# FFN input products of 512 tokens as one matmul instruction instead of two, first layer split 520 + 520, output gates for 1024 tokens

## The chip, the cores and the metric

The kernel runs on one core of one Trainium2 chip. The metric is the time of one launch on the device, in microseconds (us). Three runs of the kernel before gave 1883.02, 1883.82 and 1885.05 us; the median is 1883.82 us.

## What is computed

A trunk of one residual layer over 1024 tokens of width 1024, ahead of which 16 learned meta tokens are put (1040 tokens, dropped again at the end). All of it is float32:

```python
h = concat(meta, x)
h = h + 0.5 * rmsnorm(swiglu(rmsnorm(h, g0), w_in[0], w_out[0]), g1)      # first FFN, d_ff = 2816
h = h + rmsnorm(mlstm_mixer(rmsnorm(h, g2)), g3)                          # conv, gates, scan, output gate
h = h + 0.5 * rmsnorm(swiglu(rmsnorm(h, g4), w_in[1], w_out[1]), g5)      # second FFN
# swiglu(x): gu = x @ w_in ; (silu(gu[:, :2816]) * gu[:, 2816:]) @ w_out
```

In the mixer, the output of the scan is multiplied with sigmoid(og), og being 1024 columns of the projected input: that is the output gate. It is needed only for the 1024 real tokens.

## The kernel before

Activations stand transposed (width on the 128 partitions, tokens along the free dimension), weights are the stationary operand and tokens the moving one. Every float32 product is made of three passes on fp32r operands: each operand is split in a high part (ScalarE cast) and a low part (VectorE subtraction), and hi*hi, hi*lo and lo*hi are added in PSUM (`PASSES`, line 40).

The tokens are worked in two halves. Before the change these are A, 528 tokens (16 meta and 512 real), and B, 512 tokens, in the first FFN and the mixer, and C and E, 512 each, in the second FFN (lines 74 and 75). A matmul writes at most 512 columns, so 528 tokens go as two matmuls of 264 into the two banks of a 1024-column PSUM tile.

**The input products of an FFN** (gate and up, `x @ w_in`) are not made directly. One level of the Strassen-Winograd scheme is used: with two halves of the width, two halves of the tokens, and gate and up, each of the 22 tiles of 128 columns of d_ff takes seven products instead of eight. An operand of each product is a block of tokens, or a sum or difference of blocks of both halves of the tokens, so both halves are brought to one length; b0.n is 528 in the first FFN, with B padded with 16 zero columns (line 522), and 512 in the second. `heads` (line 428) makes two of the seven for all 22 tiles and writes them to DRAM (`hd`), while `operands` (line 494) builds the other five operands piece by piece on VectorE and ScalarE from pieces that POOL's queue loads (line 508). `joint` (line 445) loads the two back and makes the other five for each tile; VectorE adds them up, the finished activations of A leave after the fourth of them (line 484), those of B after the fifth (line 490), both by POOL's queue, into two DRAM tiles `ad[0]` and `ad[1]`. Each product is made by `product` (line 407): 4 blocks of the half width, 3 passes, and always two matmuls of n/2 columns for the two halves of n:

```python
for k in range(4):
    for pi, (wp_, xp_) in enumerate(PASSES):
        for s in range(2):
            pe.matmul(ps[:, s * 512 : s * 512 + m], lhsT=w[:, wp_, k * P : (k + 1) * P],
                      rhs=x[:, xp_, k, s * m : (s + 1) * m], ...)
    if k % 2:
        tick()
```

So one product is 24 matmuls, a layer has 22 * 7 = 154 products, and the two layers have 7392 such matmuls: 3696 of 264 columns and 3696 of 256.

**The output products** (`down`, line 560) read the activations back (`load_a`, line 553, by SP's queue, split on ScalarE and VectorE) in three segments of tiles (14 to 21, 0 to 7, 8 to 13; `SEGS`, line 238). They run for A with two matmuls of 264, for B, C and the first half of E with one of 512 or 256. The first segment of A is loaded while `joint` runs (`first_a`, line 653).

**The output gates** (`out_gates`, line 857) are eight products of 128 columns each over all tokens of a half, through `fm` (line 716): for A two matmuls of 264 for each of 24 steps, the 16 meta tokens among them, for B one of 512. Sigmoid runs on ScalarE, and POOL's queue writes the real tokens to `ogd`.

**Order of the work.** Weights come through a queue of their own, `order`: SP loads raw tiles (4 in flight), `next_w` splits them, and up to 5 split tiles stand ready. Work beside the matmuls is put in `tasks` as generators; `tick` takes one step of it, twice in each product and once in two k-steps elsewhere, so that its instructions are laid among those of the matmuls. Each engine and each queue works its instructions in order; the framework may put instructions that wait for nothing earlier than the program names them. At the start SP loads the A half of x in four pieces of two blocks (lines 623 and 627), then B's (line 640), and lines 634 to 637 build the first two operands.

Of the kernel before, what the change touches and what calls it, by code (L numbers as in the profile page):

```python
# [20 lines left out]
F32 = mybir.dt.float32  # L21
# [21 lines left out]
class Half:  # L43


    def __init__(self, i, n, meta=0, s0=0):
        self.i, self.n, self.meta, self.s0 = i, n, meta, s0
        self.subs = [(0, n)] if n <= 512 else [(0, n // 2), (n // 2, n - n // 2)]

    def part(self, s0, n):  # L50
        return Half(self.i, n, 0, self.s0 + s0)


@with_exitstack
def trunk(ctx: ExitStack, tc: tile.TileContext, xa, xb, w1, w2, w2t, g5, wqk, wv, wog, wo, par, cst, out):
    nc = tc.nc
    vec, act, pool, pe, sp = nc.vector, nc.scalar, nc.gpsimd, nc.tensor, nc.sync

# [12 lines left out]
        es = ExitStack()  # L71
        return es, es.enter_context(tc.tile_pool(name=name, bufs=bufs, reuse_waits="tile"))

    A, B = Half(0, 528, NMETA), Half(1, 512, 0)
    C, E = Half(0, 512), Half(1, 512)


    def slot(i, name):
# [13 lines left out]
    convb = pk[:, 80:88]  # L92
    ident = cp.tile([P, P], F32, name="ident")
    ones = cp.tile([P, 1], F32, name="ones")
    rn = [cp.tile([P, h.n], F32, name=f"rn{h.i}") for h in (A, B)]
    vec.memset(ones, 1.0)
    act.activation(cp.tile([P, 1], F32, name="table"), ones, AF.Silu)

    h1 = [dram.tile([P, KT, 512], F32, name=f"h1_{i}") for i in range(2)]
    h2 = [dram.tile([P, KT, 512], F32, name=f"h2_{i}") for i in range(2)]  # L100
    ad = [dram.tile([NF, P, 528], F32, name=f"a_{i}") for i in range(2)]
    hd = dram.tile([NF, 2, P, 528], F32, name="hd")
    xn = dram.tile([P, KT, 512], F32, name="xn")
    vd = dram.tile([9, P, D], F32, name="vd")
# [299 lines left out]
    def shaped(t, n):  # L404
        return t[:, :n].rearrange("p (s c) -> p s c", s=2) if n > 512 else t[:, :n]

    def product(ps, w, x, m, first):
        for k in range(4):
            for pi, (wp_, xp_) in enumerate(PASSES):
                for s in range(2):  # L410
                    pe.matmul(  # L411
                        ps[:, s * 512 : s * 512 + m],
                        lhsT=w[:, wp_, k * P : (k + 1) * P],
                        rhs=x[:, xp_, k, s * m : (s + 1) * m],
                        start=(first and k == 0 and pi == 0),
                        stop=(k == 3 and pi == 2),
                        skip_group_check=True,
                    )
            if k % 2:
                tick()  # L420

    def pv(ps, n):
        return ps.rearrange("p (s c) -> p s c", s=2)[:, :, : n // 2]

    def tv(t, n):
        return t[:, :n].rearrange("p (s c) -> p s c", s=2)

    def heads(fs, X, n, scaled):


        for f in fs:
            w = next_w()
            t, c = tmp("ht"), tmp("hc")
            x = bank("hx")
            product(x, w[0], X[0], n // 2, True)
            act.copy(tv(t, n), pv(x, n))
            pool.dma_start(hd[f, 0, :, :n], t[:, :n])
            y = bank("hy")
            product(y, w[1], X[1], n // 2, True)
            vec.tensor_tensor(tv(c, n), tv(t, n), pv(y, n), ALU.add)  # L440
            if scaled:
                act.activation(c[:, :n], c[:, :n], AF.Silu)
            pool.dma_start(hd[f, 1, :, :n], c[:, :n])

    def joint(fs, X, b0, b1, r, then):


        n = b0.n
        m = n // 2
        kept = {}  # L450

        def fetch_head(f):
            u, g = tmp("u"), tmp("g")
            sp.dma_start(u[:, :n], hd[f, 0, :, :n])
            sp.dma_start(g[:, :n], hd[f, 1, :, :n])
            kept[f] = u, g

        p = 0
        fetch_head(fs[0])
        for i, f in enumerate(fs):  # L460
            v, c = tmp("v"), tmp("c")
            u, g = kept.pop(f)
            z = bank("pz", p)
            product(z, next_w()[0], X[4], m, True)
            if r is not None:
                vec.tensor_tensor(u[:, :n], u[:, :n], r[:, :n], ALU.mult)
                vec.tensor_tensor(g[:, :n], g[:, :n], r[:, :n], ALU.mult)
                act.activation(g[:, :n], g[:, :n], AF.Silu)
            vec.tensor_tensor(tv(u, n), tv(u, n), pv(z, n), ALU.add)
            then(f, 6)  # L470
            w = bank("pw", 1 - p)
            product(w, next_w()[0], X[5], m, True)
            vec.tensor_tensor(tv(v, n), tv(u, n), pv(w, n), ALU.add)
            then(f, 7)
            if i + 1 < len(fs):
                fetch_head(fs[i + 1])
            y = bank("py", p)
            product(y, next_w()[0], X[3], m, True)
            vec.tensor_tensor(tv(v, n), tv(v, n), pv(y, n), ALU.add)
            then(f, 5)  # L480
            product(w, next_w()[0], X[6], m, False)
            vec.tensor_tensor(tv(c, n), tv(u, n), pv(w, n), ALU.add)
            vec.tensor_tensor(g[:, :n], g[:, :n], c[:, :n], ALU.mult)
            pool.dma_start(ad[0][f, :, :n], g[:, :n])
            then(f, 4)
            product(y, next_w()[0], X[2], m, False)
            vec.tensor_tensor(tv(u, n), tv(u, n), pv(y, n), ALU.add)
            act.activation(u[:, :n], u[:, :n], AF.Silu)
            vec.tensor_tensor(v[:, :n], v[:, :n], u[:, :n], ALU.mult)
            pool.dma_start(ad[1][f, :, : b1.n], v[:, : b1.n])  # L490
            then(f, 3)
            p = 1 - p

    def operands(src, b0, b1, gi, X, normed, bp, name):
# [18 lines left out]
        for k in range(4):  # L513
            for i, j in ((1, k), (1, k + 4), (0, k), (0, k + 4)):
                m = (b0, b1)[i].n
                q = t[i, j]
                if i or not normed:
                    vec.scalar_tensor_tensor(
                        q[:, :m], q[:, :m], gains[:, gi, j : j + 1], rn[i][:, :m], ALU.mult, ALU.mult)
                    yield  # L520
                if m < n:
                    vec.memset(q[:, m:n], 0.0)
                if (i, j) == (1, k + 4):
                    put(2, k, q[:, :n])
                    yield
# [24 lines left out]

    alp = [None]

    def load_a(b, fs, dst):
        for i, f in enumerate(fs):
            t = alp[0].tile([P, 528], F32, name="al", tag="al")
            sp.dma_start(t[:, : b.n], ad[b.i][f, :, : b.n])
            split_to(dst[i // 4][:, 0, i % 4, : b.n], dst[i // 4][:, 1, i % 4, : b.n], t[:, : b.n])
            yield

    def down(b, fs, a, first, load=None, each=None):  # L560
# [59 lines left out]
    sp.dma_start(pk, par)  # L620
    Z = list(range(7))
    R[0] = block(Z[5], "xa")
    sp.dma_start(R[0][:, 0:2], xa[:, 0:2])
    limit[0] = 1
    fetch()
    for k in (2, 4, 6):
        sp.dma_start(R[0][:, k : k + 2], xa[:, k : k + 2])
    limit[0] = 4
    fetch()
    sp.dma_start(ident, cst[:, 0:128])  # L630
# [1 line left out]
    X[0], X[1] = operand(Z[0], "x0_0"), operand(Z[1], "x0_1")  # L632

    for k in range(KT):
        x, g, o = R[0][:, k], gains[:, 0, k : k + 1], X[k // 4]
        act.activation(o[:, 0, k % 4], x, AF.Copy, scale=g)
        vec.scalar_tensor_tensor(o[:, 1, k % 4], x, g, o[:, 0, k % 4].bitcast(F32), ALU.mult, ALU.subtract)
    R[1] = block(Z[6], "xb")
    for k in range(0, KT, 2):
        sp.dma_start(R[1][:, k : k + 2, :512], xb[:, k : k + 2])  # L640

    def operands0():
        yield from rstd(lambda k: R[0][:, k], A.n, 1.0, "n00", [], True, rn[0])
        yield from rstd(lambda k: R[1][:, k, :512], B.n, 1.0, "n01", [], True, rn[1])
        for i in range(2, 7):
            X[i] = operand(Z[i], f"x0_{i}")
        yield from operands((xa, xb), A, B, 0, X, False, bp, "o0")

    tasks.append(operands0())
    heads(TILES, X, A.n, False)  # L650
    finish()

    def first_a(li, b, Z):
        a0 = []

        def then(f, q):
            if f == 0 and q == 6:
                a0.extend((operand(Z[0], f"a{li}_0"), operand(Z[1], f"a{li}_1")))
                tasks.append(load_a(b, SEGS[0], a0))

        return a0, then

    es_b.close()
    es_al, alp[0] = stage("al0", 2)
    a0, then = first_a(0, A, Z)
    joint(TILES, X, A, B, rn[0], then)
    finish()
    es_al.close()
    es.close()
# [23 lines left out]
    if True:  # L693
# [22 lines left out]
        def fm(h, name, every=2):  # L716
# [3 lines left out]
            for k in range(KT):  # L720
                for pi, (wp_, xp_) in enumerate(PASSES):
                    for s, (s0, m) in enumerate(h.subs):
                        pe.matmul(  # L723
                            ps[:, s * 512 : s * 512 + m],
                            lhsT=w[k // 4][:, wp_, k % 4 * P : (k % 4 + 1) * P],
                            rhs=xh[h.i][k // 4][:, xp_, k % 4, s0 : s0 + m],
                            start=(k == 0 and pi == 0),
                            stop=(k == KT - 1 and pi == 2),
                        )
# [125 lines left out]
                    tasks.appendleft(gates(h, gates_t, got))  # L855

        def out_gates(h):
            n = h.n
            for c in range(KT):
                ps = fm(h, f"wog{h.i}_{c}")  # L860
                e = tmp("oge")
                act.activation(sbv(h, e[:, :n]), psv(h, ps), AF.Sigmoid)
                pool.dma_start(
                    ogd[4 * h.i : 4 * h.i + 4, :, c].rearrange("c p t -> p c t"),
                    e[:, h.meta : n].rearrange("p (c t) -> p c t", t=P),
                )

        taken = {}
# [315 lines left out]
def _layout(inputs):  # L1184
# [4 lines left out]
    def tiles(w):  # L1189
# [17 lines left out]
    cst[0:8, [256] + [256 + 16 + 128 * c for c in range(4)]] = 0.0  # L1207
    cst[0:8, [256 + 528 + 128 * c for c in range(4)]] = 0.0
    return {
        "xa": xt[:, :, :528], "xb": xt[:, :, 528:], "w1": w1, "w2": w2,  # L1210
        "w2t": f["ffn_w_out"][0, 1].reshape(NF, P, D), "g5": f["norm_gains"][0, 5:6], "wqk": tiles(wa[:, 0:1024]), "wv": wv,
        "wog": tiles(wa[:, 2048:3072]), "wo": tiles(f["a_w_out"][0]), "par": par, "cst": cst,
    }
# [19 lines left out]
```

## Time and profile before

| what | value |
|---|---|
| median of 3 runs | 1883.82 us |
| the profiled execution | 1881.98 us, its span 1880.2 us |
| TensorE busy / weight loads busy | 1853.1 us / 1738.7 us |
| VectorE / ScalarE / GpSimd busy | 1294.1 / 768.3 / 209.8 us |
| mean granted TensorE clock | 0.998 of full speed |

The span reaches from the first to the last instruction of the profiled execution; 1.8 us of its time lie outside it. PE is TensorE's matmuls, PEld its weight loads (each matmul has one, and it overlaps the matmul ahead), DVE is VectorE, ACT ScalarE, POOL GpSimd, SP SyncE; a name with q (SPq, POOLq) is that engine's queue of DMA issues. The ends of matmuls are modelled in the profile, so that one matmul's duration includes its way through the array; the pace is read from a stretch's length over its number of matmuls. A few per cent of the matmul records can be missing, and a window's count takes in those that overlap its edges, so that counts come from the program.

### The profile page before, as it was taken

What the parts mean: (1) busy time and instruction counts of PE and PEld (TensorE: products, weight loads), DVE (VectorE), ACT (ScalarE), POOL (GpSimd) and SP (SyncE); (2) the same over time, 40 slices, a digit from 0 to 9 for tenths busy, and PEclk for the clock granted to TensorE, in tenths of its full rate; (3) what the DMA queues carried; (4) which work ended last, traced back from release to release, by engine and by line L of the source; (5) the groups of instructions that cost most, each with busy time, mean ns of one, the idle gap of its engine ahead of it and who ended that gap; (6) DMA issues with size and microseconds to landing.
All of it is one profiled execution on the core that took longest, in us unless ns stands there. A gap on an engine that the chain in (4) does not pass through costs nothing.

```text
span 1880.2 us, 34386 instructions
## 1 busy us (share of the span) xinstructions
PE 1853.1 (99%) x13556; PEld 1738.7 (92%) x13556; DVE 1294.1 (69%) x2310; ACT 768.3 (41%) x1352; POOL 209.8 (11%) x376
## 2 busy tenths in 40 slices
PE   7999999999999999999999999999999999999998
PEld 7999999999999888899789878999999999888996
DVE  6857888887356746772864577787788777545874
ACT  5433333323334423443555445564233222344553
POOL 1210000000000101301002112221000000000200
PEclk9999999999999999999999999999999999999999
DMA  8555444445346424624435546766555444554863
GB/s 311 200 202 177 165 166 153 142 145 182 116 153 192 154 79 150 194 91 139 129 109 168 180 132 228 253 230 208 163 169 174 146 160 144 180 161 142 302 203 123
DMA packets 113218, 320.23 MB, mean 170 GB/s; under 512 B 14512, under 2 KB 23152, under 8 KB 113056
## 3 DMA queue, kind: packets, MB, share of 16 engines
q1 hardware_dynamic: 84032, 223.09, 37.8%
q0 software_dynamic: 28880, 94.67, 14.1%
q8 instruction: 107, 1.75, 0.4%
q14 instruction: 55, 0.45, 0.1%
q10 hardware_dynamic: 144, 0.26, 0.0%
HBM read 248.09 MB, written 69.88 MB: 169 GB/s over the span
## 4 chain that ended last, share of the span: by engine, by line
PE 91%; issue 4%; DMA 2%; DVE 1%; ACT 1%; POOL 1%; DVEq 0%; POOLq 0%; ACTq 0%
PE pd L568 23%; PE py L411 13%; PE pw L411 13%; PE pz L411 7%; PE hy L411 6%; PE hx L411 6%; PE po L999 5%; PE wog_ps L723 5%; PE wqk_ps L723 4%; PE pv L834 4%; PE pt L1126 3%; PE pn L946 1%; DMA o<-xa 1%; DMA W<-nmd 1%; PE pn L940 0%
## 5 line engine op out<-in xcount | busy, mean ns | idle before, releaser
L568 PE MATMUL pd<-a,w 128*128 128x264 f32 (+2 forms) x2592 | 433.2, 328 | 0.0
L568 PEld LDWEIGHTS pd<-a,w 128*128 128x128 f32 x2592 | 383.7, 188 | 46.1
L411 PE MATMUL py<-x,w1j_p 128*128 128x264 f32 (+1 forms) x2112 | 266.7, 282 | 0.0
L411 PE MATMUL pw<-x,w1j_p 128*128 128x264 f32 (+1 forms) x2112 | 266.7, 282 | 0.0
L411 PEld LDWEIGHTS pw<-x,w1j_p 128*128 128x128 f32 x2112 | 258.4, 188 | 0.0
L411 PEld LDWEIGHTS py<-x,w1j_p 128*128 128x128 f32 x2112 | 258.3, 188 | 0.0
L139 ACT CAST w1j_p<-w1j_s 128x512 fp32r<-128x512 f32 x176 | 109.4, 621 | 311.9 <-PE py L411 184.3
L140 DVE TENSOR_TENSOR w<-w_raw,w 128x512 fp32r<-128x512 f32 x192 | 123.6, 646 | 122.8 <-ACT w L139 122.2
L139 ACT CAST w<-w_raw 128x512 fp32r<-128x512 f32 x192 | 111.9, 585 | 177.4 <-PE pd L568 160.6
L411 PE MATMUL hx<-x,w1a 128*128 128x264 f32 (+1 forms) x1056 | 137.5, 286 | 10.2 <-ACT w1a L139 8.1
L411 PEld LDWEIGHTS hx<-x,w1a 128*128 128x128 f32 x1056 | 131.9, 191 | 10.9 <-ACT w1a L139 8.1
L411 PE MATMUL hy<-x,w1a 128*128 128x264 f32 (+1 forms) x1056 | 135.5, 283 | 3.0 <-DVE hc L440 2.7
L411 PEld LDWEIGHTS hy<-x,w1a 128*128 128x128 f32 x1056 | 130.0, 189 | 3.7 <-DVE hc L440 3.1
L411 PE MATMUL pz<-x,w1j_p 128*128 128x264 f32 (+1 forms) x1056 | 133.4, 282 | 0.0
L140 DVE TENSOR_TENSOR w1j_p<-w1j_s,w1j_p 128x512 fp32r<-128x512 f32 x176 | 121.9, 693 | 12.1 <-ACT w1j_p L139 10.4
L411 PEld LDWEIGHTS pz<-x,w1j_p 128*128 128x128 f32 x1056 | 129.2, 188 | 0.0
L834 PE MATMUL pv<-wv,xh 128*128 128x260 f32 (+1 forms) x864 | 108.3, 286 | 0.0
L834 PEld LDWEIGHTS pv<-wv,xh 128*128 128x128 f32 (+1 forms) x864 | 102.8, 179 | 3.8 <-issue 0.3
L723 PE MATMUL wqk_ps<-xh,wqk 128*128 128x264 f32 (+1 forms) x576 | 98.0, 325 | 0.0
L999 PE MATMUL po<-xh,wo 128*128 128x512 f32 x384 | 96.3, 400 | 0.0
L723 PE MATMUL wog_ps<-xh,wog 128*128 128x264 f32 (+1 forms) x576 | 91.8, 321 | 0.0
L723 PEld LDWEIGHTS wog_ps<-xh,wog 128*128 128x128 f32 x576 | 82.6, 188 | 8.3
(371 smaller groups left out, 2372.2 us busy)
## 6 DMA issues: line engine op xcount, KB each, us to landing
w1j_raw<-w SPq DMA_DIRECT2D x88, 512.0 KB, 3.7
w_raw<-w SPq DMA_DIRECT2D x64, 512.0 KB, 3.8
w1a_raw<-w SPq DMA_DIRECT2D x43, 512.0 KB, 4.7
al<-a SPq DMA_DIRECT2D x66, 256.0 KB, 3.7
w_raw<-w SPq DMA_DIRECT2D x32, 384.0 KB, 3.3
a<-v POOLq DMA_DIRECT2D x44, 256.0 KB, 2.5
w2t_raw<-w2t SPq DMA_DIRECT2D x22, 512.0 KB, 4.3
wv_raw<-wv SPq DMA_DIRECT2D x16, 520.0 KB, 3.5
```

The lines of the kernel that those rows point to most:

```text
L139: act.copy(t[:, 0, :n], src)
L140: vec.tensor_tensor(t[:, 1, :n], src, t[:, 0, :n].bitcast(F32), ALU.subtract)
L411: pe.matmul(ps[:, s * 512 : s * 512 + m], lhsT=w[:, wp_, k * P : (k + 1) * P], rhs=x[:, xp_, k, s * m : (s + 1) * m], start=(first and k = ...
L568: pe.matmul(ps[:, s * 512 : s * 512 + m], lhsT=w[i // 4][:, wp_, i % 4 * P : (i % 4 + 1) * P], rhs=a[i // 4][:, xp_, i % 4, b.s0 + s0 : b. ...
L723: pe.matmul(ps[:, s * 512 : s * 512 + m], lhsT=w[k // 4][:, wp_, k % 4 * P : (k % 4 + 1) * P], rhs=xh[h.i][k // 4][:, xp_, k % 4, s0 : s0 ...
L834: pe.matmul(ps[:L, :VW], lhsT=xh[h.i][k // 4][:, xp_, k % 4, t0 : t0 + L], rhs=w[k // 2][:, wp_, k % 2 * VW : (k % 2 + 1) * VW], start=(k ...
L946: pe.matmul(pn[e][:, j * 129 : (j + 1) * 129], lhsT=W[:, q], rhs=v[:, q, 0:129], start=False, stop=True, skip_group_check=True)
L999: pe.matmul(ps[:, :512], lhsT=w[k // 4][:, wp_, k % 4 * P : (k % 4 + 1) * P], rhs=xh[h.i][k // 4][:, xp_, k % 4, 0:512], start=(k == 0 and ...
L1126: pe.matmul(pt[t][h], lhsT=c[g][j // 4][:, xp_, j % 4, 256 + t * P : 256 + (t + 1) * P], rhs=w[h][:, wp_, :512], start=(i == 0 and pi == 0 ...
```

## The change

`product` takes the number of tokens and makes one matmul of n columns where n is at most 512, two of n/2 above. In the first FFN the 1040 tokens are cut 520 + 520 (F and G) for the input products, without padding; the output products and the mixer keep 528 + 512 (A and B). x comes as one array of 1040 tokens, of which both cuts are views, and the activations go to one DRAM tile `ad` of 1040 tokens a row. So the last 8 tokens of A belong to G: `load_a` fetches the first segment of A with 520 tokens a row and then these 8 tokens of all 8 tiles in one DMA of POOL's queue ("edge"), with two small splits behind it. The output gates of A are made for its 512 real tokens, as one matmul of 512. The diff, cut to its core:

```diff
+    F, G = Half(0, 520), Half(1, 520, off=520)
+    A, B = Half(0, 528, NMETA), Half(1, 512, off=528)
+    C, E = Half(0, 512), Half(1, 512, off=512)
+    xa, xb = xs[:, :, : A.n], xs[:, :, A.n :]
+    xf, xg = xs[:, :, : F.n], xs[:, :, F.n :]
...
-    ad = [dram.tile([NF, P, 528], F32, name=f"a_{i}") for i in range(2)]
+    ad = dram.tile([NF, P, T], F32, name="ad")
...
-    def product(ps, w, x, m, first):
+    def product(ps, w, x, n, first):
+        subs = 1 if n <= 512 else 2
+        m = n // subs
         for k in range(4):
             for pi, (wp_, xp_) in enumerate(PASSES):
-                for s in range(2):
+                for s in range(subs):
                     pe.matmul(
...
-            pool.dma_start(ad[0][f, :, :n], g[:, :n])
+            pool.dma_start(ad[f, :, :n], g[:, :n])
...
-            pool.dma_start(ad[1][f, :, : b1.n], v[:, : b1.n])
+            pool.dma_start(ad[f, :, n : 2 * n], v[:, :n])
...
-                if m < n:
-                    vec.memset(q[:, m:n], 0.0)
...
-    def load_a(b, fs, dst):
+    def load_a(b, fs, dst, n=None):
+        n = n or b.n
         for i, f in enumerate(fs):
             t = alp[0].tile([P, 528], F32, name="al", tag="al")
-            sp.dma_start(t[:, : b.n], ad[b.i][f, :, : b.n])
-            split_to(dst[i // 4][:, 0, i % 4, : b.n], dst[i // 4][:, 1, i % 4, : b.n], t[:, : b.n])
+            sp.dma_start(t[:, :n], ad[f, :, b.off : b.off + n])
+            split_to(dst[i // 4][:, 0, i % 4, :n], dst[i // 4][:, 1, i % 4, :n], t[:, :n])
+            yield
+        if n < b.n:
+            for _ in range(4):
+                yield
+            t = st.tile([P, len(fs), b.n - n], F32, name="edge", tag="edge", bufs=1)
+            pool.dma_start(t, ad[fs[0] : fs[-1] + 1, :, b.off + n : b.off + b.n].rearrange("f p t -> p f t"))
+            yield
+            for j in range(0, len(fs), 4):
+                o = dst[j // 4][:, :, :, n : b.n]
+                split_to(o[:, 0], o[:, 1], t[:, j : j + 4])
             yield
...
-    sp.dma_start(R[0][:, 0:2], xa[:, 0:2])
+    sp.dma_start(R[0][:, 0:2, : F.n], xf[:, 0:2])
...
-        sp.dma_start(R[1][:, k : k + 2, :512], xb[:, k : k + 2])
+        sp.dma_start(R[1][:, k : k + 2, : G.n], xg[:, k : k + 2])
...
-        yield from operands((xa, xb), A, B, 0, X, False, bp, "o0")
+        yield from operands((xf, xg), F, G, 0, X, False, bp, "o0")
...
-    heads(TILES, X, A.n, False)
+    heads(TILES, X, F.n, False)
...
-    a0, then = first_a(0, A, Z)
-    joint(TILES, X, A, B, rn[0], then)
+    a0, then = first_a(0, A, Z, F.n)
+    joint(TILES, X, F, G, rn[0], then)
...
-                            rhs=xh[h.i][k // 4][:, xp_, k % 4, s0 : s0 + m],
+                            rhs=xh[h.i][k // 4][:, xp_, k % 4, h.s0 + s0 : h.s0 + s0 + m],
...
         def out_gates(h):
-            n = h.n
+            q, n = Half(h.i, 512, 0, h.meta), 512
             for c in range(KT):
-                ps = fm(h, f"wog{h.i}_{c}")
+                ps = fm(q, f"wog{h.i}_{c}")
                 e = tmp("oge")
-                act.activation(sbv(h, e[:, :n]), psv(h, ps), AF.Sigmoid)
+                act.activation(e[:, :n], psv(q, ps), AF.Sigmoid)
```

The reading of PSUM follows (`pv` and `tv` take one block of n columns where n is at most 512), and the first two normalizing rows, the loops over x at the start and the operands of the first FFN are 520 wide instead of 528 and 512.

## Rows read from the trace of the kernel before

**Rows 1.** The page: span and busy time of each engine.

```profile
span 1880.2 us, 34386 instructions
...
PE 1853.1 (99%) x13556; PEld 1738.7 (92%) x13556; DVE 1294.1 (69%) x2310; ACT 768.3 (41%) x1352; POOL 209.8 (11%) x376
```

**Rows 2.** Stretches: length, busy PE, PEld, DVE, ACT, POOL (instructions), PEclk, DMA share, GB/s.

```profile
8.00:34.50 26.50, 23.96 (x165) 22.93 (x166) 19.59 (x39) 17.27 (x33) 2.72 (x5) 1.00 0.99 386
34.50:83.40 48.90, 46.20 (x377) 45.56 (x376) 41.31 (x78) 23.49 (x42) 11.94 (x22) 1.00 0.64 214
...
150.90:471.57 320.67, 320.67 (x2643) 320.67 (x2641) 268.17 (x402) 105.64 (x169) 23.32 (x43) 1.00 0.49 161
...
1309.41:1619.82 310.41, 310.41 (x2643) 310.41 (x2642) 239.83 (x358) 92.57 (x149) 23.86 (x44) 1.00 0.51 166
...
1619.82:1742.26 122.44, 122.44 (x531) 99.15 (x530) 60.69 (x95) 49.33 (x86) 2.04 (x4) 1.00 0.48 149
...
839.70:886.32 46.62, 46.62 (x385) 46.62 (x385) 14.52 (x23) 15.85 (x26) 5.29 (x7) 1.00 0.44 133
...
1140.80:1158.49 17.69, 17.69 (x79) 14.35 (x78) 17.48 (x28) 11.50 (x22) 4.55 (x7) 1.00 0.56 188
...
977.00:1012.90 35.90, 35.90 (x301) 35.90 (x301) 15.04 (x43) 14.94 (x30) 6.78 (x13) 1.00 0.51 163
```

**Rows 3.** PE in order of time (start, us): the mixer's output product, line 999.

```profile
1140.80 17.85 PE L999 MATMUL po<-xh,wo 128*128 128x512 f32 x76
```

**Rows 4.** PE's groups by shape (busy us, mean ns | idle before, releasers): heads, first FFN.

```profile
L411 PE MATMUL hx<-x,w1a 128*128 128x264 f32 x528 | 71.7, 292 | 10.2 <-ACT w1a L139 8.1 <-ACT x L636 2.0
L411 PE MATMUL hy<-x,w1a 128*128 128x264 f32 x528 | 69.2, 286 | 3.0 <-DVE hc L440 2.7 <-DVE x L637 0.2
```

**Rows 5.** PE in order of time, heads of the first FFN; idle time in brackets.

```profile
69.23 3.16 PE L411 MATMUL hy<-x,w1a 128*128 128x264 f32 x24 [0.43 <-DVE hc L440]
...
83.41 3.20 PE L411 MATMUL hy<-x,w1a 128*128 128x264 f32 x24 [2.27 <-DVE hc L440]
```

**Rows 6.** The chain that ended last, one step in the same stretch.

```profile
73.77 5.61 DMA o<-xa
```

**Rows 7.** POOL's DMA issues: by line, then in order of time, ninth tile of joint.

```profile
L863 POOL DMA_DIRECT2D ogd<-oge x16 | 12.1, 759 | 105.5 <-ACT oge L862 105.5
...
267.11 0.54 POOL L484 DMA_DIRECT2D a<-g  x1 [10.38 <-DVE g L483]
270.74 0.54 POOL L490 DMA_DIRECT2D a<-v  x1 [3.09 <-DVE v L489]
```

**Rows 8.** DMA issues by line: KB each, median us to landing.

```profile
a<-v POOLq DMA_DIRECT2D x44, 256.0 KB, 2.5
...
g<-hd SPq DMA_DIRECT2D x22, 264.0 KB, 4.1
a<-g POOLq DMA_DIRECT2D x22, 264.0 KB, 3.7
...
xa<-xa SPq DMA_DIRECT2D x4, 528.0 KB, 11.8
```

**Rows 9.** PE in order of time, then the stretch around it: the granted clock dips.

```profile
773.75 6.06 PE L834 MATMUL pv<-wv,xh 128*128 128x260 f32 x36
...
727.00:793.00 66.00, 64.03 (x520) 60.02 (x518) 51.35 (x123) 29.72 (x62) 23.24 (x43) 0.97 0.59 185
```

**Rows 10.** What the DMA queue of SP waited for (us, times, longest).

```profile
SPq L556 <- DMA a<-g: 75.2, 16, 5.1
```

**Rows 11.** SP's queue, then DVE, in order of time, second tile of joint.

```profile
167.42 0.33 SPq L556 DMA_DIRECT2D al<-a  x1
...
169.26 0.37 SPq L455 DMA_DIRECT2D g<-hd  x1
...
175.75 0.70 DVE L467 TENSOR_TENSOR g<-g,rn 128x528 f32<-128x528 f32 x1
```

More of the change, by code (lines that the diff above doesn't have):

```diff
@@ L43, with __init__, trunk @@
 class Half:
-    def __init__(self, i, n, meta=0, s0=0):
-        self.i, self.n, self.meta, self.s0 = i, n, meta, s0
+    def __init__(self, i, n, meta=0, s0=0, off=0):
+        self.i, self.n, self.meta, self.s0, self.off = i, n, meta, s0, off
         self.subs = [(0, n)] if n <= 512 else [(0, n // 2), (n // 2, n - n // 2)]
     def part(self, s0, n):
-        return Half(self.i, n, 0, self.s0 + s0)
+        return Half(self.i, n, 0, self.s0 + s0, self.off)
 @with_exitstack
-def trunk(ctx: ExitStack, tc: tile.TileContext, xa, xb, w1, w2, w2t, g5, wqk, wv, wog, wo, par, cst, out):
+def trunk(ctx: ExitStack, tc: tile.TileContext, xs, w1, w2, w2t, g5, wqk, wv, wog, wo, par, cst, out):
     nc = tc.nc
@@ L72, in stage @@
         return es, es.enter_context(tc.tile_pool(name=name, bufs=bufs, reuse_waits="tile"))
-    A, B = Half(0, 528, NMETA), Half(1, 512, 0)
-    C, E = Half(0, 512), Half(1, 512)
+    F, G = Half(0, 520), Half(1, 520, off=520)
[3 more added lines that the diff above has]
+    xf, xg = xs[:, :, : F.n], xs[:, :, F.n :]
     def slot(i, name):
@@ L94, in trunk @@
     ones = cp.tile([P, 1], F32, name="ones")
-    rn = [cp.tile([P, h.n], F32, name=f"rn{h.i}") for h in (A, B)]
+    rn = [cp.tile([P, h.n], F32, name=f"rn{h.i}") for h in (A, G)]
     vec.memset(ones, 1.0)
@@ L422, in pv @@
     def pv(ps, n):
-        return ps.rearrange("p (s c) -> p s c", s=2)[:, :, : n // 2]
+        return ps[:, :n] if n <= 512 else ps.rearrange("p (s c) -> p s c", s=2)[:, :, : n // 2]
     def tv(t, n):
-        return t[:, :n].rearrange("p (s c) -> p s c", s=2)
+        return shaped(t, n)
     def heads(fs, X, n, scaled):
@@ L434, in heads @@
             x = bank("hx")
-            product(x, w[0], X[0], n // 2, True)
+            product(x, w[0], X[0], n, True)
             act.copy(tv(t, n), pv(x, n))
@@ L438, in heads @@
             y = bank("hy")
-            product(y, w[1], X[1], n // 2, True)
+            product(y, w[1], X[1], n, True)
             vec.tensor_tensor(tv(c, n), tv(t, n), pv(y, n), ALU.add)
@@ L448, in joint @@
         n = b0.n
-        m = n // 2
         kept = {}
@@ L463, in joint @@
             z = bank("pz", p)
-            product(z, next_w()[0], X[4], m, True)
+            product(z, next_w()[0], X[4], n, True)
             if r is not None:
@@ L471, in joint @@
             w = bank("pw", 1 - p)
-            product(w, next_w()[0], X[5], m, True)
+            product(w, next_w()[0], X[5], n, True)
             vec.tensor_tensor(tv(v, n), tv(u, n), pv(w, n), ALU.add)
@@ L477, in joint @@
             y = bank("py", p)
-            product(y, next_w()[0], X[3], m, True)
+            product(y, next_w()[0], X[3], n, True)
             vec.tensor_tensor(tv(v, n), tv(v, n), pv(y, n), ALU.add)
             then(f, 5)
-            product(w, next_w()[0], X[6], m, False)
+            product(w, next_w()[0], X[6], n, False)
             vec.tensor_tensor(tv(c, n), tv(u, n), pv(w, n), ALU.add)
             vec.tensor_tensor(g[:, :n], g[:, :n], c[:, :n], ALU.mult)
-            pool.dma_start(ad[0][f, :, :n], g[:, :n])
+            pool.dma_start(ad[f, :, :n], g[:, :n])
             then(f, 4)
-            product(y, next_w()[0], X[2], m, False)
+            product(y, next_w()[0], X[2], n, False)
             vec.tensor_tensor(tv(u, n), tv(u, n), pv(y, n), ALU.add)
@@ L626, in trunk @@
     for k in (2, 4, 6):
-        sp.dma_start(R[0][:, k : k + 2], xa[:, k : k + 2])
+        sp.dma_start(R[0][:, k : k + 2, : F.n], xf[:, k : k + 2])
     limit[0] = 4
@@ L634, in trunk @@
     for k in range(KT):
-        x, g, o = R[0][:, k], gains[:, 0, k : k + 1], X[k // 4]
+        x, g, o = R[0][:, k, : F.n], gains[:, 0, k : k + 1], X[k // 4][:, :, :, : F.n]
         act.activation(o[:, 0, k % 4], x, AF.Copy, scale=g)
@@ L639, in trunk, with first_a @@
     for k in range(0, KT, 2):
-        sp.dma_start(R[1][:, k : k + 2, :512], xb[:, k : k + 2])
+        sp.dma_start(R[1][:, k : k + 2, : G.n], xg[:, k : k + 2])
     def operands0():
-        yield from rstd(lambda k: R[0][:, k], A.n, 1.0, "n00", [], True, rn[0])
-        yield from rstd(lambda k: R[1][:, k, :512], B.n, 1.0, "n01", [], True, rn[1])
+        yield from rstd(lambda k: R[0][:, k, : F.n], F.n, 1.0, "n00", [], True, rn[0])
+        yield from rstd(lambda k: R[1][:, k, : G.n], G.n, 1.0, "n01", [], True, rn[1])
         for i in range(2, 7):
             X[i] = operand(Z[i], f"x0_{i}")
-        yield from operands((xa, xb), A, B, 0, X, False, bp, "o0")
+        yield from operands((xf, xg), F, G, 0, X, False, bp, "o0")
     tasks.append(operands0())
-    heads(TILES, X, A.n, False)
+    heads(TILES, X, F.n, False)
     finish()
-    def first_a(li, b, Z):
+    def first_a(li, b, Z, n=None):
         a0 = []
@@ L658, in then @@
                 a0.extend((operand(Z[0], f"a{li}_0"), operand(Z[1], f"a{li}_1")))
-                tasks.append(load_a(b, SEGS[0], a0))
+                tasks.append(load_a(b, SEGS[0], a0, n))
         return a0, then
@@ L857, in out_gates @@
         def out_gates(h):
-            n = h.n
+            q, n = Half(h.i, 512, 0, h.meta), 512
             for c in range(KT):
-                ps = fm(h, f"wog{h.i}_{c}")
+                ps = fm(q, f"wog{h.i}_{c}")
                 e = tmp("oge")
-                act.activation(sbv(h, e[:, :n]), psv(h, ps), AF.Sigmoid)
+                act.activation(e[:, :n], psv(q, ps), AF.Sigmoid)
                 pool.dma_start(
                     ogd[4 * h.i : 4 * h.i + 4, :, c].rearrange("c p t -> p c t"),
-                    e[:, h.meta : n].rearrange("p (c t) -> p c t", t=P),
+                    e[:, :n].rearrange("p (c t) -> p c t", t=P),
                 )
@@ L1209, in _layout @@
     return {
-        "xa": xt[:, :, :528], "xb": xt[:, :, 528:], "w1": w1, "w2": w2,
+        "xs": xt, "w1": w1, "w2": w2,
         "w2t": f["ffn_w_out"][0, 1].reshape(NF, P, D), "g5": f["norm_gains"][0, 5:6], "wqk": tiles(wa[:, 0:1024]), "wv": wv,
```

## The prediction

> **What bounds the kernel now.** I read the page's busy times first. TensorE is busy for 1853.1 of 1880.2 us, no other engine for more than 69% [rows 1]. The reader should see that only 27 us of the span are not matmul, so a change pays by making the matmul stream shorter or not at all. But busy matmul time says nothing on pace, so the second view is the table of stretches, in which I divide the length of a stretch by the matmuls that the program has in it; the count behind a window may take in up to three at its edges. The first joint stage is 22 tiles of 5 products of 24 matmuls, 2640 of 264 columns in 320.67 us: 121.46 ns each. The second has 2640 of 256 in 310.41 us: 117.58 ns. The output products of C are 528 of 512 in 122.44 us: 231.9 ns. The output gates of A, 384 of 264, take 46.62 us: 121.4 ns [rows 2]. The mixer's output product runs 76 of 512 in 17.69 us: 232.8 ns [rows 2, 3].
>
> In the joint stages PE is busy to the last hundredth while VectorE stands at 84% and 77%: nothing makes the matmuls wait there, whatever ends a product's VectorE work. Two things follow. A matmul's time is nearly proportional to its columns: from 256 to 512 the pace rises by 114.3 ns for 256 columns, 0.447 ns a column, which leaves 3.2 ns fixed for each. So halving the number of matmuls at the same columns saves little, and dropping columns saves in proportion. The heads of the first FFN are the exception: their two groups have 13.2 us of idle time before them, 10.2 and 3.0, most of it at the start [rows 4].
>
> **First FFN, 264 to 260 columns.** The 3696 matmuls stay, each with 4 columns fewer. What 260 columns take is in the trace, in another product: 300 matmuls of the mixer's values in 35.90 us, 119.67 ns [rows 2]. From the two neighbours 264 and 256 the middle is 119.52. By the clock alone, 4 columns at 2.4 GHz are 1.67 ns. The savings are 1.79, 1.94 and 1.67 ns a matmul, times 3696: 6.6, 7.2 and 6.2 us. I take 6.6, the row with the very width, and keep 6.2 and 7.2 as ends.
>
> **Second FFN, two of 256 to one of 512.** 3696 matmuls become 1848. A pair now takes 235.16 ns. One of 512 takes 231.9 where VectorE is 50% busy and 232.8 where it is 99% busy [rows 2, 3]; the second FFN lies between, at 77% in the joint stage. So each saves 3.27 to 2.36 ns: 6.0 to 4.4 us, and I take 5.2.
>
> The Trainium skill, in "TensorE: Matmul & The Clock Gate", section "Back-to-back issue gap", gives the isolated gap as N/2.4 + 2.5 ns, so 215.8 for 512 and 109.2 for 256; the traces here are slower, at 231.9 and 117.58, so its level doesn't hold. By its fixed 2.5 ns this part would save 4.6 us, as an estimate, inside the ends above.
>
> **Output gates of A.** 384 of 264 in 46.62 us become 192 of 512, of which 16 columns a row fewer: 192 times 232.35, the middle of the two paces, is 44.6, so 2.0 us. Sigmoid on ScalarE runs on 512 instead of 528 columns, beside the matmuls. B's gates are as before.
>
> **What the start and the heads keep.** Until 34 us the DMA engines are 99% busy, and PE waits for x and the weights [rows 2, 4]. Between 34.5 and 83.4 us PE still waits 2.7 us in all: at 83.41 for the addition hc on VectorE, 2.27 us, and at 69.23, 0.43 us [rows 2, 5]. VectorE had waited for a piece of x that POOL asked for at 73.77 and that landed 5.61 us later [rows 6]. A shorter product doesn't bring that piece sooner, so here the wait grows by what the matmuls save: the 16 products from 34 to 83 us, at 24 * 1.79 ns each, lose 0.7 us again.
>
> **Edits that I cost at nothing.** The first load of x brings pieces of 520 columns cut out of rows of 1040, so that its two blocks no longer lie in one piece; a load of 528 KB lands after 11.8 us while the engines are saturated [rows 2, 8]. The bytes fall by 1.5% there and rise by as much in the second half. I take 0, with ends of a tenth of a microsecond gained and 1 us lost. Memsets that are dropped and VectorE work of 520 instead of 528 columns lie under the matmuls.
>
> The edge DMA is new: 8 tiles times 128 rows, 1024 pieces of 32 bytes, on POOL's queue. The nearest row is the write of the output gates, 512 pieces in an issue of 0.759 us; a plain one of 128 pieces takes 0.54 [rows 7]. It is needed only when the joint stage ends at 471 us, about 200 us after the ninth tile starts. Behind it on POOL waits the next write of g, for which the queue sits idle 10 us anyway [rows 7]. Its reads come behind the last write of v, which lands in 2.5 us [rows 8]. If the small splits on ScalarE and VectorE stand in front of other work when the DMA is late, that costs once; with a write, an issue and a load of about 3 us the bound is 3 us, and 0 is likelier, since five split weights stand ready. Loads of A's later segments now span what two writes left, but they come in the output stage, behind both.
>
> In the mixer, 36 matmuls of 260 took 6.06 us at 773.75, where 119.67 ns each would be 4.3: the granted clock of that stretch is 0.97, a short drop from 2.4 to 1.2 GHz behind a wait of PE [rows 9]. If the new timing moves the waits, this 1.7 us may go or come twice.
>
> **Sum.** 6.6 + 5.2 + 2.0 - 0.7 = 13.1 us of the profiled execution's 1881.98 us, 0.70%. That execution is 1.8 us below the median of 1883.82, so the same share gives 1870.7 us.
>
> **Rivals.**
>
> *Columns alone set the pace.* If one of 512 takes as long as two of 256 once it stands in this stage, the second FFN gives nothing and the output gates 46.62 - 192 * 0.2352 = 1.5 us: 6.6 + 1.5 - 0.7 = 7.4 us, 1876.4. Against it: the same shape ran at 232.8 ns beside a VectorE at 99% [rows 2, 3]. Chance 0.07.
>
> *The weight loads set the pace of the halves.* PEld is busy in every hundredth of the 264 and 256 stretches and 81% of the 512 stretch [rows 2]. If the load is the limit of a short matmul, dropping 4 columns gives nothing and only fewer loads pay: 5.2 + 2.0 = 7.2 us, 1876.6. Against it: the same load of 128x128 goes with 121.46 and with 117.58 ns, 3.9 ns for 8 columns, so the columns do count. Chance 0.05. It is the Trainium skill, "Perfetto Trace Analysis", section "Identifying the Most-Contended Engine", that has one judge TensorE by the busy share of weight loads; the 3.9 ns speak against that reading here.
>
> *The loads of a hold SP's queue.* This one ends slower. Loads of the first segment wait in SP's queue for the write of g, 16 times for 75.2 us, up to 5.1 us each [rows 10]; behind them stand the loads of u and g of the next tile and the raw weights. With one DRAM tile for both halves they might be held until v of that tile, or a later write, has landed. By the rows, v leaves 3.6 us after g and lands 1.2 us faster, so the load would go some 2.4 us later. The load of g now goes at 169.26, lands after 4.1 us and is used at 175.75: 2.4 us to spare [rows 8, 11]. So up to there it costs nothing, and beyond it VectorE stands, which has 16% free. To make the kernel slower by more than 0.2%, the 16 loads must cost 13.1 + 3.8 = 17 us, 1.06 us each after VectorE's free 2.3 us a tile: held some 5.8 us longer than now. Then the time is 1888 or more. The columns of the two writes don't overlap, and the load takes only g's, so I give it 0.04.
>
> **The numbers.** Forecast 0.81, columns alone 0.07, weight loads 0.05, SP's queue 0.04, and 0.03 for an end within 0.2%, with some of the held loads but not all. 0.2% is about what a measurement of this kernel can tell from no change, 3.8 us. The ends of the forecast: 7.2 + 6.0 + 2.1 - 0.7 + 1.7 = 16.3 us, and 6.2 + 4.4 + 1.9 - 0.7 less the 1, 3 and 1.7 of start, edge and clock = 6.1. The last three won't come together; the two rivals with a smaller gain lie at 1876.4 and 1876.6. So the range is 1866.5 to 1876.8. Faster has the forecast and the two small gains, 0.93; same 0.03; slower 0.04.
>
> **What would show it.** The two joint stages should take 2640 * 119.67 = 316 us and 1320 * 232.35 = 306.7 us, with PE busy throughout; the gates of A 44.6 us. PEld should fall to about 81% in the second FFN. The wait of PE near 83 us should stay or grow. Wrong would be: 512 at 235 ns or more in line 411's groups, 260 at 121 ns, idle time before pz, pw or py with DVE as releaser, or waits of SP's line for `al` on the write of v.

## The result and the profile after

The changed kernel takes 1872.53 us in the median of four runs (1871.71 to 1874.24); the kernel before took 1884.43 us beside it (four runs, 1883.02 to 1885.77). The ratio is 0.9940, with a 95% interval of 0.9928 to 0.9951: 11.9 us faster, where 13.1 had been forecast, and inside the range. The profiled execution takes 1872.58 us with a span of 1870.8, 9.4 us less than the one before.

The page of the kernel after, against [rows 1]:

```profile
span 1870.8 us, 30311 instructions
...
PE 1842.5 (98%) x11520; PEld 1638.3 (88%) x11520; DVE 1292.5 (69%) x2304; ACT 767.2 (41%) x1355; POOL 210.1 (11%) x377
```

2036 matmuls fewer: 1848 in the second FFN and 192 in the gates are gone, and four more came with the normalizing rows of the first FFN, whose second half now has 520 tokens and ends in a short piece, as the first did. PE is busy 10.6 us less, and the idle time is 28.3 instead of 27.1 us: what the matmuls gave, the span got, less some 1 us.

The stretches of the kernel after, each from the first matmul of a stage to the first of the next (columns as in [rows 2]): first joint stage, second joint stage, gates of A, scan of A up to B's gates, and the 300 matmuls of the values.

```profile
150.24:468.97 318.73, 317.38 (x2643) 317.10 (x2641) 265.09 (x403) 104.65 (x171) 24.16 (x44) 1.00 0.49 162
1305.16:1611.17 306.01, 306.01 (x1321) 247.84 (x1320) 239.93 (x359) 92.66 (x149) 24.06 (x45) 1.00 0.51 168
837.38:881.90 44.52, 44.52 (x194) 36.05 (x193) 14.51 (x23) 15.75 (x26) 5.28 (x7) 1.00 0.44 138
881.90:1010.60 128.70, 126.63 (x911) 109.74 (x910) 84.43 (x222) 68.00 (x125) 12.76 (x23) 0.99 0.39 124
974.32:1010.36 36.04, 36.04 (x304) 36.04 (x303) 15.20 (x43) 15.09 (x30) 6.76 (x13) 1.00 0.50 161
```

The second row is clean: 1320 matmuls in 306.01 us are 231.8 ns each, PE busy throughout, and the weight loads down from all of the stretch to 81% of it. The first row isn't: PE was idle for 1.35 us, and the pace is not the one forecast. The whole, cut at the first matmul of each stage, in us:

| stage | before | after | difference |
|---|---|---|---|
| start and heads of the first FFN | 150.91 | 150.24 | -0.67 |
| first joint stage | 320.66 | 318.73 | -1.93 |
| output products of the first FFN | 255.27 | 255.29 | +0.02 |
| values, keys and queries of A | 112.69 | 113.12 | +0.43 |
| output gates of A | 46.63 | 44.52 | -2.11 |
| scan of A, up to B's gates | 126.99 | 128.70 | +1.71 |
| B's gates to the mixer's output | 168.46 | 168.57 | +0.11 |
| heads of the second FFN | 127.80 | 125.99 | -1.81 |
| second joint stage | 310.41 | 306.01 | -4.40 |
| output products of the second FFN and end | 260.38 | 259.63 | -0.75 |

The second FFN gives 6.2 us, the gates 2.1, the first FFN 2.6 where 5.9 was expected (6.6 less 0.7), and the scan, whose work is unchanged, takes 1.7 back. Where PE waited, in order of time (kernel after; idle time in brackets):

```profile
82.35 4.67 PE L419 MATMUL hy<-x,w1a 128*128 128x260 f32 x24 [2.48 <-DVE hc L448]
...
278.53 3.10 PE L419 MATMUL py<-x,w1j_p 128*128 128x260 f32 x24 [1.35 <-DVE v L486]
...
921.50 0.68 PE L963 MATMUL pn<-keep,W 128*128 128x129 f32 x4 [2.07 <-ACT wqk L144]
```

The first answers to [rows 5]: the wait is 2.48 us instead of 2.27, and the 24 matmuls behind it take 4.67 us instead of 3.20. Stretches around the first and the third of these waits show why; the third number from the end is the granted clock, as a mean over the stretch:

```profile
82.00:87.00 5.00, 4.65 (x26) 4.66 (x27) 5.00 (x9) 2.88 (x6) 1.07 (x2) 0.66 0.46 178
919.00:926.00 7.00, 4.93 (x23) 3.69 (x23) 5.36 (x12) 4.49 (x8) 0.00 (x0) 0.76 0.00 0
```

Before, the same two stretches stood at 1.00. So behind each of the two waits the clock fell from 2.4 to 1.2 GHz for a while, which cost 1.5 us at 82 us (4.67 against 3.20), and most of the 1.7 us of the scan at 921 us.

The wait at 278 us is new. Who waited for whom between 270 and 282 us in the kernel after (us in total, times, longest):

```profile
ACT a L331 <- DMA edge<-ad: 5.1, 1, 5.1
DVE a L332 <- ACT a L331: 4.2, 1, 4.2
POOL edge L570 <- DMA ad<-v: 4.2, 1, 4.2
...
PE py L419 <- DVE v L486: 1.3, 1, 1.3
```

POOL's edge DMA stands behind the write of v for 4.2 us, the small ScalarE split stands 5.1 us for the DMA, VectorE 4.2 us for ScalarE, and the addition that frees py's bank comes late. The matmuls behind the wait of 1.35 us ran at a granted clock of 1.00. SP's queue, against [rows 10], is as it was:

```profile
SPq L563 <- DMA ad<-g: 72.5, 16, 5.3
```

### The profile page after: what moved, and what is told of

Read it like the earlier page. It is cut to its first block, busy times and chain, and to the rows that moved or that the text cites. A ratio compares the mean times of both kernels' runs of the same rounds, so it can differ in the third digit from the quotient of the medians.

```text
span 1870.8 us, 30311 instructions
## 1 busy us (share of the span) xinstructions
PE 1842.5 (98%) x11520; PEld 1638.3 (88%) x11520; DVE 1292.5 (69%) x2304; ACT 767.2 (41%) x1355; POOL 210.1 (11%) x377
## 4 chain that ended last, share of the span: by engine, by line
PE 81%; issue 12%; DMA 2%; POOL 2%; DVE 2%; ACT 1%; SPq 0%; POOLq 0%; DVEq 0%; ACTq 0%
PE pd L585 23%; PE py L419 11%; PE pw L419 11%; PE pz L419 5%; PE po L1016 5%; PE wog_ps L740 5%; PE hx L419 4%; PE hy L419 4%; PE wqk_ps L740 4%; PE pv L851 4%; PE pt L1143 3%; PE pn L963 1%; DMA W<-nmd 1%; DMA xa<-xs 1%; PE pn L957 1%
## 5 line engine op out<-in xcount | busy, mean ns | idle before, releaser
L419 PE MATMUL py<-x,w1j_p 128*128 128x260 f32 (+1 forms) x1584 | 263.6, 320 | 1.3 <-DVE v L486 1.3
L419 PE MATMUL pw<-x,w1j_p 128*128 128x260 f32 (+1 forms) x1584 | 263.5, 320 | 0.0
L419 PEld LDWEIGHTS py<-x,w1j_p 128*128 128x128 f32 x1584 | 229.0, 188 | 24.8 <-ACT w1j_p L144 1.5
L419 PEld LDWEIGHTS pw<-x,w1j_p 128*128 128x128 f32 x1584 | 229.0, 188 | 23.3
L419 PE MATMUL hx<-x,w1a 128*128 128x260 f32 (+1 forms) x792 | 135.1, 324 | 10.6 <-ACT w1a L144 7.6
L419 PE MATMUL hy<-x,w1a 128*128 128x260 f32 (+1 forms) x792 | 135.5, 325 | 2.5 <-DVE hc L448 2.5
L419 PEld LDWEIGHTS hx<-x,w1a 128*128 128x128 f32 x792 | 116.5, 191 | 22.7 <-ACT w1a L144 7.5
L419 PE MATMUL pz<-x,w1j_p 128*128 128x260 f32 (+1 forms) x792 | 131.8, 320 | 0.0
L145 DVE TENSOR_TENSOR w1j_p<-w1j_s,w1j_p 128x512 fp32r<-128x512 f32 x176 | 121.9, 693 | 11.7 <-ACT w1j_p L144 9.4
L419 PEld LDWEIGHTS pz<-x,w1j_p 128*128 128x128 f32 x792 | 114.5, 188 | 11.7
L740 PE MATMUL wog_ps<-xh,wog 128*128 128x512 f32 x384 | 89.7, 394 | 0.0
L740 PEld LDWEIGHTS wqk_ps<-xh,wqk 128*128 128x128 f32 x576 | 81.5, 189 | 7.6 <-issue 0.5
```

What stands on the lines that cost most here:

```text
L145: vec.tensor_tensor(t[:, 1, :n], src, t[:, 0, :n].bitcast(F32), ALU.subtract)
L740: pe.matmul(ps[:, s * 512 : s * 512 + m], lhsT=w[k // 4][:, wp_, k % 4 * P : (k % 4 + 1) * P], rhs=xh[h.i][k // 4][:, xp_, k % 4, h.s0 + s ...
```

## The experiments

Stage times below are read as in the table above, and the diffs are cut to their core. The first seven kernels ran once each, beside the kernel before (1883.81 and 1886.15 us). Single executions of unchanged stages of the mixer differ by 2 us and more (the scan took 126.96 to 130.44 us), so parts are compared by stage.

### The output gates alone

```diff
-            n = h.n
+            q, n = Half(h.i, 512, 0, h.meta), 512
```

> The kernel before with the output gates of A alone changed (512 tokens, one matmul). Theory (pace by columns): the gates of A take 192 * 231.9 ns = 44.5 us instead of 46.6, nothing before them moves, so the heads and joint stages of both FFNs stay at 320.7 us and 310.4 us in their joint parts. The stretch from the end of these gates to the start of B's gates was 127.0 us before and 128.7 us after the whole change; if the earlier end of the gates brought that on, it is about 128.7 us here too and the whole gains some 0.4 us; if it came from elsewhere it stays at 127.0 and the whole gains 2.1 us. Rival (weight loads set the pace of short matmuls): the same time for the gates, since their number of loads is halved as well.

Measured: gates of A 44.52 us, both joint parts where they were (320.65 us, and 311.46 with one wait of 0.66 us on VectorE). The whole took 1882.01 us. The scan stretch took 128.85 us, which by the wording above would lay its 1.7 us to the earlier end of the gates. The next run forbids that.

### The one-instruction product alone

```diff
-                for s in range(2):
+                for s in range(subs):
```

> The kernel before with the one-instruction product alone, which touches only the second FFN. Theory (a pair of 256 takes 235.2 ns, one of 512 takes 231.8): heads 127.8 to 126.0 us, joint 310.4 to 306.0 us, 6.2 us less in all, and the first FFN as before (joint 320.7 us). Rival (the gain of the second FFN hangs on the shorter stages ahead of it): less than 5 us or a joint stage above 307 us.

Measured: heads 126.00, joint 306.01 us, the first joint stage 320.65: the theory to a tenth of a microsecond. The whole took 1879.73 us, 4.1 less than the kernel before beside it and not 6.2: in its profile two unchanged stages are some 2 us longer than in the profile of before, the output stage of the second FFN, with a wait of 2.32 us and slow matmuls behind it, and the scan. The scan stretch, ahead of which nothing had changed, took 128.64 us, with a slow piece behind a wait of 2.06 us (kernel with the product alone):

```profile
925.99 1.20 PE L948 MATMUL pn<-keep,W 128*128 128x129 f32 x4 [2.06 <-ACT wqk L139]
926.84 2.06 PE L725 MATMUL wqk_ps<-xh,wqk 128*128 128x512 f32 x4
```

Four matmuls of 512 take some 1.1 us at full clock. So the 1.7 us of the scan belong to the execution: they come without any change ahead of it. The length of the wait alone doesn't decide it: 1.86 us in the kernel before brought no drop, nor did 2.25 and 2.23 us in two kernels below (the edge held back, the second buffer), whose scan took 127.3 us.

### Where the 260 columns lose: cuts of 256 + 264, and a second half kept at column 264

```diff
-                        rhs=x[:, xp_, k, s * m : (s + 1) * m],
+                        rhs=x[:, xp_, k, s0:s1],          # cuts 0:256 and 256:520
```

> The changed kernel with the 520 tokens of the first FFN cut 256 + 264 instead of 260 + 260. Theory A (a matmul whose tokens start off at column 260 is slower) and theory B (a width of 260 is slower, wherever it starts) both give a pair of 117.58 + 121.46 = 239.0 ns where 260 + 260 took 240.3: joint stage of the first FFN 1320 * 239.0 = 315.5 us plus its one wait of 1.35 us, 316.9 us where it was 318.7, and about 0.5 us less in the heads: 2.3 us gained. Rival C (the pace is a smooth function of columns and 260 is no special case): no change, 318.7 us.

```diff
-                        rhs=x[:, xp_, k, s * m : (s + 1) * m],
+                        rhs=x[:, xp_, k, s * 264 : s * 264 + m],
```

> The changed kernel with both halves still 260 columns wide, but the second half kept from column 264 of the operand on, not from 260. Theory A (start at column 260 is what costs): 119.5 ns a matmul, joint stage 315.5 plus the wait of 1.35 = 316.9 us. Theory B (width of 260): 120.14 ns as after the change, joint stage 318.7 us.

The joint stages took 322.09 and 319.09 us (the whole 1874.57 and 1877.05), with waits of 1.86 and 1.41 us behind the edge; behind the first of these the clock fell too (0.66 over 5 us), and 24 matmuls took 4.58 us. The pace shows in undisturbed products, here the first and the last start of 21 of them, for the cut 256 + 264, then for the second half at column 264 (in the first, the form shown is one of the products' two, 256 and 264):

```profile
198.12 3.06 PE L418 MATMUL py<-x,w1j_p 128*128 128x256 f32 x24
...
258.92 3.06 PE L418 MATMUL pw<-x,w1j_p 128*128 128x256 f32 x24
```

```profile
197.98 3.05 PE L419 MATMUL pw<-x,w1j_p 128*128 128x260 f32 x24
...
258.56 3.05 PE L419 MATMUL py<-x,w1j_p 128*128 128x260 f32 x24
```

60.80 us for 21 products of 12 pairs are 241.3 ns a pair, and 60.58 are 240.4; the changed kernel has 240.2 (2.882 us a product in the same stretch). So the start at column 260 costs nothing, theory A falls, and 256 + 264 is slower than 260 + 260, which none of the three expected: a matmul of 256 keeps its 117.58 ns among its like, and a pair of unlike ones is no mean of the two. Why is open.

### 512 + 8: what a short matmul costs

```diff
-        subs = 1 if n <= 512 else 2
+        cuts = [(0, 0, n)] if n <= 512 else [(0, 0, 512), (512, 512, n)]
```

> The changed kernel with the 520 tokens of the first FFN cut 512 + 8. Theory (3.2 ns fixed and 0.447 ns a column, for any width): a pair takes 231.8 + 6.8 = 238.6 ns instead of 240.2, joint stage 315.0 plus the wait of 1.35 = 316.3 us. Rival (a short matmul can't be quicker than its weight load, which runs beside the matmul ahead of it): the pair pays the load of the next matmul that 8 columns can't cover. The nearest rows of short matmuls with a load of their own are 16 of 128 columns in 1.09 us, 68 ns: 300 ns a pair or more, joint stage 396 us or more.

The kernel took 2072.6 us. Its first joint stage:

```profile
215.61:669.24 453.63, 453.63 (x2643) 395.08 (x2641) 268.88 (x405) 104.74 (x171) 24.78 (x45) 1.00 0.34 113
```

453.63 us for 1320 pairs are 343.7 ns, 111.8 more than one of 512 alone. Eight columns cost nearly as much as 256. The weight loads of this trace bear out the rival: within a pair they start 108 ns apart, and nowhere in the stage closer, so a pair takes the time of 512 columns and about one load more. The rule of a fixed 3.2 ns holds only where the next weight load is covered; the load is a floor. The 68 ns of the expectation came from loads of 64 rows (pss), which start in pairs 7 ns apart and are no measure of a load of 128 rows. At 256 and 264 columns, 117.6 and 121.5 ns, the kernel was above that floor, but not by much. The Trainium skill, "TensorE: Matmul & The Clock Gate", section "LDWEIGHTS (loading the stationary operand)", gives a load of P columns P / 1.2 ns, by which 128 columns would take 106.7 ns, as an estimate. The 108 and 111.8 ns here agree with it within 5%.

### The edge's splits held back

```diff
-            yield
+            for _ in range(16):
+                yield
+            last = mark[0]                                 # the Silu of the newest tile
...
-                split_to(o[:, 0], o[:, 1], t[:, j : j + 4])
+                i = act.copy(o[:, 0], t[:, j : j + 4])     # ordered behind it on ScalarE
+                vec.tensor_tensor(o[:, 1], t[:, j : j + 4], o[:, 0].bitcast(F32), ALU.subtract)
```

> The changed kernel with the two small ScalarE splits of the edge held back in ScalarE's order behind the Silu of a tile three tiles later; the DMA and the work are the same. Theory (the splits stood in ScalarE's queue waiting 5.07 us for the edge DMA, VectorE 4.21 us behind them, and PE 1.35 us behind VectorE): no idle time of PE before py in the first joint stage, which takes 2640 * 120.1 = 317.1 us instead of 318.7. Rival (the wait comes from VectorE's load in that tile, not from the edge): the idle time stays at 1.3 us or moves to the tile where the splits now stand.

The first joint stage of this kernel:

```profile
151.55:468.56 317.01, 317.01 (x2643) 317.01 (x2641) 266.35 (x404) 104.83 (x171) 24.23 (x44) 1.00 0.49 163
```

No idle time is left (the whole took 1870.34 us), and 317.01 us are 120.08 ns a matmul: the edge cost 1.7 us, 1.35 of idle time and the rest in slower matmuls behind it.

### A second buffer in the heads

```diff
-                                  bufs=1 if (i, j // 4) == (0, 1) else 2)
+                                  bufs=2)
...
-            if k < 3:
-                load(0, k + 5)
...
+            if k in (1, 2):
+                load(0, k + 5)                             # ahead of block k; (0, 5) with block 0's loads
```

> The changed kernel with a second buffer for the pieces of the first token half's upper blocks in the heads stage (the helper tile t1 comes from the pool of temporaries, to make room), and the load asked for one block earlier. Theory (PE's idle 2.48 us at 82 us, and the drop of the granted clock behind it, come from a piece that is asked for only when its one buffer is free): that idle time goes, the 24 matmuls behind it take 3.0 instead of 4.67 us by the profile, and the heads of the first FFN end some 4 us sooner, at about 146.3 us. Rival (the DMA engines or VectorE set it): the idle time stays above 1.5 us or moves to another product of that stage, and the heads end within 1 us of 150.2.

The stretch where PE had waited and run slowly, in this kernel, and the one wait that remains ahead of it:

```profile
70.00:90.00 20.00, 20.00 (x167) 20.00 (x168) 16.52 (x27) 8.27 (x15) 6.52 (x12) 1.00 0.69 235
```

```profile
69.89 3.13 PE L419 MATMUL hy<-x,w1a 128*128 128x260 f32 x24 [0.99 <-DVE hc L448]
```

The wait at 82 us and the drop are gone; 0.99 us of waiting came up at 69.9 us. The heads end at 147.81 us, 2.4 us sooner than in the changed kernel's first profile, not the 3.9 expected; the whole took 1868.73 us. The edit has two parts, the second buffer and the earlier load, and no run tells them apart.

### Both, against the changed kernel

> The changed kernel with both: the edge's splits held back, and the second buffer in the heads stage. Theory (the two waits are independent, 1.6 us and 2.4 us in the profiles of the two alone): first joint stage 317.0 us, heads about 147.8 us, and some 4 us less than the changed kernel in the same rounds: about 0.9916 of the kernel before. Rival (a wait removed early comes back later in another form): within 1.5 us of the changed kernel.

> The changed kernel as it is, beside the one above on the same chip: 0.9935 to 0.994 of the kernel before. Its profile tells what varies from one execution to the next: the second FFN (126.0 and 306.0 us), the gates of A (44.5 us) and the output stages should be the same to 0.1 us, the waits near 82, 278, 772, 778 and 921 us and the drops of the granted clock behind them need not be.

Five rounds on one chip: the kernel before 1884.01 us, the changed kernel 1874.20 us (ratio 0.9943, 0.9931 to 0.9956), with both edits 1866.38 us (0.9901, 0.9886 to 0.9917), which beats both. That is 7.8 us less than the changed kernel, more than the 4 expected. In the two profiles the heads differ by 3.9 us (151.40 and 147.54) and the joint stage by 1.7 (318.75 and 317.01), 5.6 us for the two edits, and 1.7 more lie in a wait of the mixer (2.54 and 0.62 us at its normalizing row), a wait that also varies between executions without these edits. The stages that were to be the same are: 126.00 and 125.98, 306.01 and 306.02, 44.52 and 44.52. The stretch of the heads in this profile of the changed kernel:

```profile
83.40:88.40 5.00, 4.96 (x28) 4.96 (x29) 5.00 (x9) 2.84 (x6) 1.07 (x2) 0.66 0.43 163
```

The drop of the clock came here again, behind a wait of 2.17 us: the 24 matmuls took 4.63 us. The same product starts at 81.26 us with both edits instead of 83.44, and takes 3.04 us: together 3.8 us, nearly all of the 3.9 by which the heads differ.

The drop in the heads is in every profile of products of 260 + 260 with the one buffer: these two, the edge held back, and the second half at column 264 (a wait of 2.69 us, then 24 matmuls in 4.53). It is in none of the three kernels with 264 + 264, though their waits were about as long in two, and not in the cut 256 + 264, behind a wait of 1.83 us. The kernel with the edge held back, then the one with the product alone:

```profile
83.68 4.65 PE L419 MATMUL hy<-x,w1a 128*128 128x260 f32 x24 [2.38 <-DVE hc L448]
```

```profile
83.55 3.17 PE L414 MATMUL hy<-x,w1a 128*128 128x264 f32 x24 [2.23 <-DVE hc L443]
```

So the drop here, unlike the one in the scan, may be a cost of the change; no run settles it. With the drop the heads gain nothing in the mean: they end at 150.24, 151.40 and 151.55 us in the three profiles with the changed kernel's heads, and at 150.91, 150.88 and 151.04 us in the three with the old ones.

## Why the prediction was right, and where it was not

**What bounds the kernel.** Right. The gain came out of the pace of matmuls, stage by stage.

**Second FFN.** Right in its mechanism, a little beyond the better end: 6.2 us for the forecast 5.2 and the ends of 4.4 and 6.0. One of 512 takes 231.8 ns there, beside a VectorE 78% busy, as the 231.9 beside one 50% busy [rows 2]; the middle between the two paces was too careful.

**Output gates.** Right: 2.1 us for 2.0.

**First FFN, 264 to 260 columns.** This is the step that failed in size. The 1.79 ns a matmul rested on 119.67 ns, from a window of 35.90 us [rows 2] that began a little behind the first of its 300 matmuls. From the start of the first to the start of the next stage's they take 36.04 us, in the kernel after as before: 120.1 ns, and 120.08 is what the joint stage shows once the edge is out of the way. So the term should have been 1.38 * 3696 = 5.1 us and not 6.6, outside the ends of 6.2 and 7.2 as well. The 1.67 ns by the clock alone didn't hold either. The middle between 256 and 264 was no bound either.

**The start and the heads.** The forecast loss of 0.7 us was right in kind: the wait at 83 us stayed, at 2.48 us. What it left out is the drop of the clock behind it, 1.5 us in the profile, which together with the wait takes, in the mean of the profiles, all that the shorter products gain in this stage. (Between 34 and 83 us the trace has 15 products and not 16, a difference of 0.04 us.) The drop had been considered only for the place where the trace of before showed one [rows 9].

**Edits costed at nothing.** The edge had a bound of 3 us and was taken as 0; it cost 1.7 us, by just the way that the bound named, splits that stand in front of other work while the DMA is late. The argument for 0, five split weights standing ready, covers the weights but not the additions that free the banks, and VectorE was behind ScalarE in the same wait. Idle time before py with DVE as releaser was one of the prediction's own signs of being wrong, and it came. The load of x in smaller pieces, POOL's queue and the later segments cost nothing that can be seen.

**The rivals.** Columns alone: fell, the pair of 256 became 3.3 ns cheaper. Weight loads: fell as the bound of the halves, since 264 to 260 gained 1.38 ns at the same number of loads, though a floor of some 110 ns is real. SP's queue: fell, its waits for g are 72.5 us in 16 times as before, and none for v.

By its terms as measured, the change gives 6.2 + 2.1 + 5.1 = 13.4 us of pace, less 1.7 for the edge: 11.7 us. The two profiles are 9.4 us apart: there the heads of the first FFN give 0.7 instead of 1.5 us, the unchanged stages of the mixer take 2.2 more, and the last output stage 0.8 less. The medians are 11.9 us apart in the first four rounds and 9.8 in the five later ones, so that single waits and drops weigh as much as a term of the sum. That the total came within 1.2 us of the forecast is in part luck: the second FFN gave 1.0 more than forecast, the first 3.3 less in its profile, and the execution of before that was profiled lay 2.4 us below the median of the four runs beside the change.

## What to carry to other kernels

Take a pace from the start of one matmul to the start of another, never from a window set by hand: an error of 0.14 us in 36 was 1.5 us in the sum. Fewer and longer matmuls save what lies beyond the columns, here 3.3 ns a pair, and short leftovers cost a whole weight load, so it can pay to cut equal halves. The splits of a tiny transfer belong well behind its landing in the queue of every engine that they pass; that their result is needed late is not enough.

## What the runs showed that was not expected

A pair of 256 + 264 columns takes 241.3 ns, more than two of 260 (240.2) and more than the mean of its own two widths (239.0). And a wait of PE of 2 us may or may not be followed by some microseconds at 1.2 GHz: in the scan, waits of 1.71, 1.91 and 2.06 us were followed by a drop and waits of 1.86, 2.23 and 2.25 us were not; in the heads, 2.17, 2.38, 2.48 and 2.69 us were, all with products of 260 + 260, and 2.23 and 2.27 us with 264 + 264 were not. So the length alone doesn't decide; what does is not settled by these runs.
